# Two edits to a hybrid attention layer: table copies at another place, softmax reciprocals on another engine

## The chip, the cores and the metric

The kernel runs on one core of a Trainium2 chip. A core has a matrix engine (TensorE, PE in the profile, with its weight loads on a row of their own, PEld), three engines for elementwise work (VectorE, DVE; ScalarE, ACT; GpSimd, POOL) and a queue that issues transfers (SyncE, SP). The engines run side by side, each through its own instructions in a fixed order, and wait for each other by semaphores. Operands lie in an on-chip memory of 128 partitions. Matmul results go to a small memory of their own, PSUM, which the kernel uses as eight banks of 128 x 512 numbers. GpSimd does not touch PSUM in this kernel.

The metric is the time of one execution on the device in microseconds, as the median of the runs.

## The reference

Two decoder layers over 512 tokens of width 1024. Each layer projects its input once, and the columns feed two groups of heads and an indexer. Cut to what matters here:

```python
h = x @ w_in
qa, ka, va, qb, kb, vb, qi, ki, wi = split(h)
qa, ka, qb, kb, qi, ki = rope(...)            # ki after a layer norm of its own
# group A: window of 128 keys, a learned sink per head in the sum
m  = max(s.max(-1), sink)
pr = exp(s - m)
denom = pr.sum(-1) + exp(sink - m)
oa = einsum(pr / denom, v)
# group B: an index score picks 128 keys per query, then a softmax over these
idx_score = sum_h(relu(qi . ki) * wi), causal
sel = top_k(idx_score, 128)
ob = softmax(s over sel) @ v
mix = concat(oa, ob) @ w_o
x = layer_norm(alpha * x + mix)
x = layer_norm(alpha * x + (silu(x @ wg) * (x @ wu)) @ w_down + sigmoid(x @ w_pg) * (p @ w_pp))
```

`rope` turns pairs of columns by the cosine and sine of position times frequency. There are 8 query heads in each group, 8 index heads, and 2 layers.

## The kernel before

All matmuls are made of three products of a number split in two parts (high times high, high times low, low times high: `mm3`, L332 to L336). So every weight tile that arrives by a transfer (`wst`) is split before use: ScalarE rounds it to the high part (L256, L280, L287) and GpSimd subtracts that to get the low part (L257, L281, L288). The split tiles `wsp` have five buffers, and when TensorE is done with one (`w_rel`), the next is split and the next transfer issued (`w_pump`).

The tokens are four blocks of 128, `t` = 0 to 3. A layer runs through these stages:

- `start()` (L845): for each `t` the 296 columns of the indexer are projected (L865), and `gi_out` (L564) turns and splits the index queries and normalises the index key. Then the 384 key and value columns for blocks (0, 1) and (2, 3) (L868, `kv_out` at L605). Then `turned_tables()` (L869, L627). Then the first two query groups of A, `queries` (L833), whose results `q_out` (L640) turns with the turned tables.
- beside it `index()` (L670): for `t` = 1 to 3 and each of eight heads one product (L677), a relu on ScalarE (L679) and a weighted sum on VectorE (L680).
- then `rest()` (L873): the query groups of B and the first half of the output projection, beside `attention()` (L785) and `topk()` (L685, 16 rounds of the eight largest, L691 and L692, for each `t` from 1).
- the output projection's other half, the feed-forward part and the gated embedding, up to the next layer.

**The table copies.** The rotary table `tab64` holds, for each token (on partitions), 32 cosines and 32 sines, twice each. It is made once, at the start, by `rotary()` (L462 to L500). The queries come out of TensorE with columns on partitions, so each layer needs the table turned. `turned_tables()` copies for cosine and for sine the 32 columns four times side by side for each block (`wide`, L632, ScalarE, 128 x 512), turns the four blocks on TensorE into a PSUM bank (L636) and copies that to `cs` (L637). `wide` is one of the twelve buffers of the pool `t2k`. `cs` is read first by `q_out` (L645).

**The reciprocals.** `scores()` (L698) handles one unit: a group, a block `t` and four heads. After the products (L716), VectorE adds the mask and takes the negative maximum (L720), and ScalarE takes the exponential with its sum into `sums`, 128 x 4 (L724). For group A GpSimd makes the sink's exponent (L727), ScalarE its exponential (L728), and GpSimd adds it to `sums` (L729). Then VectorE takes the reciprocal (L730) and GpSimd copies it out to 64 columns per head (`rb`, L732). `values()` (L735) turns the exponentials (L753, copied by L755), multiplies by the values (L747), turns `rb` (L764, copied by L767) and multiplies the two (L772). `AHEAD = 2`: the values of a unit stand beside the scores of the unit two later. There are 16 units in a layer.

**What sets the order.** The Python program emits the work of each stage as several generators that `Order.run` (L67) interleaves by written-out costs. `order.later` puts transposes some cost units behind what feeds them (`D_K = 8.0` for the keys, L620 and L622; `D_GI` for the index queries, L532 and L533). The framework then takes the emitted instructions with their place in the program as priority, assigns buffers and banks (`bank`, L113: eight, shared by all), and fixes for each engine the order in which it runs its instructions. So an instruction emitted earlier may be put earlier on its engine, but at run time each engine goes through its list in order. `tc.issue_after` ties some to others.

Of the kernel before, what the change touches and what calls it, by code (L numbers as in the profile page):

```python
# [10 lines left out]
F32 = mybir.dt.float32  # L11
# [4 lines left out]
OP = mybir.AluOpType  # L16
# [4 lines left out]
NT = S // 128  # L21
# [75 lines left out]
def hybrid_kernel(ctx: ExitStack, tc: tile.TileContext, x, p, positions, ln_in_g, ln_in_b, w_in,  # L97
# [3 lines left out]
    PE, V, A, G, SP = nc.tensor, nc.vector, nc.scalar, nc.gpsimd, nc.sync  # L101
# [6 lines left out]
    small = ctx.enter_context(tc.tile_pool(name="small", bufs=4))  # L108
# [4 lines left out]
    def bank(tag, bufs, dt=F32):  # L113
        return psum.tile([128, 512], dt, name="bank", tag="bank", bufs=8)

    def acc():
        return bank("acc", 4)
# [4 lines left out]
    def t2k(dt=F32):  # L122
        return tmp.tile([128, 512], dt, name="t2k", tag="t2k")
# [23 lines left out]
    idf = const.tile([128, 128], F32, name="idf")  # L147
# [74 lines left out]
    def w_dma(i):  # L222
        if wq[i][0] == "op":
            return
        if wq[i][0] == "raw":
            _, w, f = wq[i]
            for q in ("11", "12", "21", "22"):
                h = int(q[1]) - 1
                quarter[q] = [slot(F32) for _ in range(2)]
                for j in range(2):  # L230
                    r = (2 * (f + j) + int(q[0]) - 1) * 128
                    SP.dma_start(quarter[q][j], w[r:r + 128, h * 512:(h + 1) * 512])
            return
        a, cols, _ = wq[i]
        n = sum(ap.shape[1] for ap in cols)
        st = wst.tile([128, 1024], F32, name="wst", tag="wst")
        sv = st[:, :a * n].rearrange("p (a n) -> p a n", a=a)
        o = 0
        for ap in cols:
            SP.dma_start(sv[:, :, o:o + ap.shape[1]], ap.rearrange("(a p) n -> p a n", p=128))  # L240
            o += ap.shape[1]
        wst_live[i] = st
        if i in X_AT:
            load_x(X_AT[i])
# [59 lines left out]
    def w_pump():  # L304
        while True:
            go = False
            staged = sum(e[0] != "op" for e in wq[wpos["split"]:wpos["dma"]])
            if wpos["dma"] < len(wq) and staged < ST_AHEAD:
                w_dma(wpos["dma"])
                wpos["dma"] += 1  # L310
                go = True
            i = wpos["split"]
            if i < wpos["dma"] and (wpos["room"] or wq[i][0] == "raw" or wq[i][2] is True and wq[i][0] != "op"):
                w_split(i)
                wpos["split"] += 1
                go = True
            if not go:
                return

    def w_take():  # L320
        i = wpos["use"]
        if wq[i][0] == "raw":
            i += 1
        wpos["use"] = i + 1
        assert i in w_live, (i, wpos)
        return w_live.pop(i)

    def w_rel():
        wpos["room"] += 1
        w_pump()  # L330
# [21 lines left out]
    for i in range(4):  # L352
        ps = bank("gb", 4)
# [3 lines left out]
    def tok(t):  # L357
        return slice(t * 128, (t + 1) * 128)
# [95 lines left out]
    tab64 = const.tile([128, NT, 2, 64], F32, name="tab64")  # L454
# [7 lines left out]
    def rotary():  # L462
# [33 lines left out]
        for tab, f0, h in ((tab64, 0, 32), (tab32, 32, 16)):  # L496
# [2 lines left out]
            A.copy(tab[:, :, 1, :h], s3[:, :, f0:f0 + h])  # L499
            G.tensor_scalar(tab[:, :, 1, h:], s3[:, :, f0:f0 + h], -1.0, 1.0, op0=OP.mult, op1=OP.mult)  # L500

    w_pump()
    ln_in(0)
    table = rotary()
# [36 lines left out]
    def take(n):  # L541
        return [w_take() for _ in range(n)]

    def project(ws, n, blocks, lhs, done, rel=0):

        ks = [(i, r, len(w[0])) for i, w in enumerate(ws) for r in range(len(w[0]))]
        ps = [acc() for _ in blocks]
        for k, (i, r, a) in enumerate(ks):
            for o, t in zip(ps, blocks):
                mm3(o[:, :n], *lhs(t, k), ws[i][0][r], ws[i][1][r], k == 0, k == len(ks) - 1)  # L550
            if i < rel and r == a - 1:
                w_rel()
            yield 3 * len(blocks) * 0.218 * n / 512
        for o, t in zip(ps, blocks):
            done(t, o)

    for l in range(L):
# [1 line left out]
        kiT = slot()  # L559
        qiT, qT, work, wi, vt, ma = {}, {}, {}, {}, {}, {}  # L560
        ready = set()
        kin, kmv, turned = {}, {}, []

        def gi_out(t, ps):  # L564

# [39 lines left out]
        def kv_out(t, ps):  # L605
# [18 lines left out]
                order.tick(0.4)  # L624
            order.later(D_K, turns)

        def turned_tables():  # L627

            cs = const.tile([128, D], F32, name="lng", tag="lng")
            for i in range(2):  # L630
                wide = t2k()
                A.copy(wide.rearrange("p (t n i) -> p t n i", t=NT, n=4),  # L632
                       tab64[:, :, i, None, :32].to_broadcast([128, NT, 4, 32]))
                ps = bank("tp", 2)
                for t in range(NT):
                    PE.transpose(ps[:, tok(t)], wide[:, tok(t)], idf)  # L636
                A.copy(cs[:, i * 512:(i + 1) * 512], ps)  # L637
            return cs[:, :512], cs[:, 512:]

# [58 lines left out]
        def scores(kind, t, g, st):  # L698
            if kind == "a":
                k0, nk, c = max(0, t - 1) * 128, (256 if t else 128), g  # L700
                mask = win if t else win[:, 128:]
                yield from wait((kind, t, g), *[("k", b) for b in range(max(2, t + 1))])
            else:
                k0, nk, c = 0, (t + 1) * 128, 2
                yield from wait((kind, t, g), *[("k", b) for b in range(max(2, t + 1))], *[("s", t)] * (t > 0))
                mask = work[t] if t else causal[:, S - 128:]
            nn = max(nk, 256)
            per = 512 // nn
            ng, sums = sm(4, "ng"), sm(4, "sums")
            es = []  # L710
            for j in range(4):
                if j % per == 0:
                    ps, e = bank("sc", 2), t2k()
                o = j % per * nn
                for s in range(2):
                    PE.matmul(ps[:, o:o + nn], qT[kind, g][j][:, tok(t)], kT[c, s][:, k0:k0 + nn],  # L716
                              start=(s == 0), stop=(s == 1))
                es.append(e[:, o:o + nk])
                far = nsink[:, l, 4 * g + j:4 * g + j + 1] if kind == "a" else 3e38
                V.tensor_tensor_reduce(es[j], ps[:, o:o + nk], mask, -HD ** -0.5, far, op0=OP.add, op1=OP.min,  # L720
                                       accum_out=ng[:, j:j + 1])
                yield 0.44 * nn / 512
            for j in range(4):
                A.activation(es[j], es[j], AF.Exp, bias=ng[:, j:j + 1], scale=-1.0, accum_out=sums[:, j:j + 1])  # L724
            if kind == "a":
                ek = sm(4, "ek")
                G.tensor_tensor(ek, sink[:, l, 4 * g:4 * g + 4], ng, OP.add)  # L727
                A.activation(ek, ek, AF.Exp)  # L728
                G.tensor_tensor(sums, sums, ek, OP.add)  # L729
            V.reciprocal(sums, sums)  # L730
            rb = small.tile([128, 256], F32, name="rb", tag="rb", bufs=3)
            G.tensor_copy(rb.rearrange("p (j d) -> p j d", j=4), sums[:, :, None].to_broadcast([128, 4, 64]))  # L732
            st.extend([es, rb, k0 // 128, nk // 128])
# [111 lines left out]
        def start():  # L845
            ws = take(3)
            for t in range(NT):
                if l == 0 or t == 3:
                    to_features(t)
                    yield 0.9  # L850
                if l == 0 and t == 0:
                    with tc.issue_after(last["copy"]):
                        ln_in_sums(2)
                    ln_in_sums(3)
                    for _ in table:
                        pass
                if l == 0 and t + 1 < NT:
                    ln_in(t + 1)
                done = gi_out
                if l == 0 and t + 1 < NT:  # L860
                    done = behind(last["norm"], gi_out)
                if l == 0 and t == 2:
                    with tc.issue_after(last["norm"]):
                        V.tensor_scalar(nsink, sink, -1.0, None, op0=OP.mult)
                yield from project(ws, 296, (t,), from_f, done, 3 * (t == 3))  # L865
            ws = take(4)
            for b in ALL:
                yield from project(ws, 384, b, from_f, kv_out, 4 * (b is ALL[-1]))  # L868
            turned.extend(turned_tables())  # L869
            for q in QS[:NSTART]:  # L870
                yield from queries(*q)
# [133 lines left out]
        for gi, fs in enumerate(GROUPS):  # L1005
            hs = []
            for f in fs:
# [7 lines left out]
                if gi == 1 and f == fs[0]:  # L1015
                    pT = {}
                    for k in range(2):
                        ps = bank("tp", 2)
# [14 lines left out]
            for h in range(2):  # L1033
                ps = [acc() for _ in range(NT)]
                n = len(hs)
# [13 lines left out]
        for b in TAIL:  # L1049
            for h in range(2):  # L1050
# [4 lines left out]
                ps = [acc() for _ in b]  # L1055
# [52 lines left out]
```

## Time and profile before

| | us |
|---|---|
| median of 3 runs | 1276.74 (1276.61 to 1277.25) |
| the profiled execution's own time | 1275.16 |
| its span in the profile | 1273.4 |
| TensorE busy in the span | 1223.8 |
| GpSimd busy in the span | 677.9 |

The profile shows one execution; times in it are microseconds from the start of its span. A row of its timeline gives start, duration, engine, line of the kernel, operation, output and inputs, shapes and count (neighbouring instructions of one kind are merged), and in brackets how long the engine was idle before and what it waited for. A row of the table by stretches gives for each engine the busy time and the number of instructions, then the granted TensorE clock (1.00 is full), the share of the transfer engines and what they moved. A table of waits gives who waited for whom, the total, how often, and the longest. A row for a line of the kernel gives the shortest, median and longest duration of its instructions in ns, and when the first and the last started. Matmuls overlap, so their durations are longer than the distance from one to the next.

### The profile page before, as it was taken

To read this page: it belongs to the slowest core of one execution; us is meant where nothing else is said; L and a number is where in the kernel's file an instruction comes from. 1 tells how busy PE (TensorE), PEld (TensorE's weight loads), DVE (VectorE), ACT (ScalarE), POOL (GpSimd) and SP (SyncE) were. 2 spreads that over 40 slices of the span, in tenths; PEclk is the share of its full clock that TensorE was granted. 3 is DMA by queue.
4 is the path that set the end of the run, shared out by engine and by line. 5 is a ranking of instruction groups with operands and counts; after the bars stand their busy time and mean duration, and the time that the engine had idled before them with its cause. 6 is when DMAs were issued, how large, how long until landed. Compare 5 with 4: busy or idle time off the path is not lost.

```text
span 1273.4 us, 17210 instructions
## 1 busy us (share of the span) xinstructions
PE 1223.8 (96%) x6056; PEld 1006.3 (79%) x6056; DVE 773.4 (61%) x1678; ACT 583.4 (46%) x1185; POOL 677.9 (53%) x523
## 2 busy tenths in 40 slices
PE   7889999999999999999997989999999999999996
PEld 5877667888888888888896867679888888888885
DVE  7689953773636363726677997556736363645365
ACT  6557774443434343434335766843434342434331
POOL 6856632366565656562166645324756575747400
PEclk9989999999999999999998989999999999999998
DMA  5324241343242323034032433204242423231321
GB/s 174 85 82 118 76 155 35 99 131 115 69 132 74 125 77 121 17 116 138 13 91 79 126 90 92 108 27 155 85 132 67 132 79 120 84 99 42 108 83 50
DMA packets 95406, 121.09 MB, mean 95 GB/s; under 512 B 7508, under 2 KB 68180, under 8 KB 95320
## 3 DMA queue, kind: packets, MB, share of 16 engines
q1 hardware_dynamic: 94648, 119.97, 30.4%
q8 instruction: 47, 0.77, 0.3%
q14 instruction: 39, 0.32, 0.1%
q10 hardware_dynamic: 672, 0.03, 0.0%
HBM read 109.49 MB, written 2.10 MB: 88 GB/s over the span
## 4 chain that ended last, share of the span: by engine, by line
PE 83%; DVE 5%; ACT 4%; POOL 4%; issue 2%; DMA 2%; SPq 0%; DVEq 0%; ACTq 0%; POOLq 0%
PE bank L334 25%; PE bank L335 25%; PE bank L336 25%; PE bank L747 2%; PE bank L716 2%; PE bank L753 2%; DMA wst<-in_w_pg_dram 1%; POOL wsp L288 1%; POOL wsp L281 1%; DVE t2k L720 1%; ACT t2k L724 1%; POOL slot L526 1%; PE bank L447 1%; DVE slot L273 1%; PE bank L764 1%
## 5 line engine op out<-in xcount | busy, mean ns | idle before, releaser
L288 POOL TENSOR_TENSOR wsp<-wst,wsp 128x1024 fp32r<-128x1024 f32 (+2 forms) x132 | 313.1, 2385 | 252.2 <-ACT wsp L287 250.2
L335 PE MATMUL bank<-fl,wsp 128*128 128x512 f32 (+1 forms) x896 | 336.0, 376 | 0.4 <-DVE fl L450 0.4
L334 PE MATMUL bank<-fh,wsp 128*128 128x512 f32 (+1 forms) x896 | 335.1, 377 | 1.0 <-ACT fh L449 1.0
L336 PE MATMUL bank<-fh,wsp 128*128 128x512 f32 (+1 forms) x896 | 334.2, 375 | 0.0
L287 ACT CAST wsp<-wst 128x1024 fp32r<-128x1024 f32 (+2 forms) x132 | 134.8, 1030 | 181.2 <-PE bank L336 132.7
L334 PEld LDWEIGHTS bank<-fh,wsp 128*128 128x128 f32 x896 | 168.5, 189 | 31.6 <-ACT fh L449 1.9
L335 PEld LDWEIGHTS bank<-fl,wsp 128*128 128x128 f32 x896 | 169.4, 189 | 30.0 <-DVE fl L450 0.9
L336 PEld LDWEIGHTS bank<-fh,wsp 128*128 128x128 f32 x896 | 169.3, 189 | 29.7
L914 DVE TENSOR_TENSOR t2k<-bank,t2k 128x512 f32<-128x512 f32 x44 | 30.4, 692 | 222.2 <-PE bank L336 222.2
L257 POOL TENSOR_TENSOR wsp<-slot,wsp 128x512 fp32r<-128x512 f32 x100 | 141.4, 1440 | 28.9 <-ACT wsp L256 28.9
L334 PE MATMUL bank<-wsp,slot 128*128 128x512 f32 x392 | 153.3, 391 | 0.0
L335 PE MATMUL bank<-wsp,slot 128*128 128x512 f32 x392 | 152.7, 390 | 0.0
L336 PE MATMUL bank<-wsp,slot 128*128 128x512 f32 x392 | 148.0, 389 | 0.0
L822 DVE TENSOR_TENSOR x<-bank,x 128x512 f32<-128x512 f32 x140 | 91.5, 686 | 88.5 <-PE bank L336 88.5
L944 ACT CAST slot<-t2k 128x256 fp32r<-128x256 f32 (+1 forms) x104 | 49.9, 498 | 143.7 <-DVE t2k L914 102.1
L257 POOL TENSOR_TENSOR wsp<-t2k,wsp 128x512 fp32r<-128x512 f32 x40 | 57.5, 1449 | 92.7 <-ACT wsp L256 92.7
L334 PE MATMUL bank<-wsp,fh 128*128 128x512 f32 (+2 forms) x256 | 92.2, 364 | 1.1 <-ACT fh L449 0.8
L336 PE MATMUL bank<-wsp,fl 128*128 128x512 f32 (+2 forms) x256 | 91.4, 360 | 1.5 <-DVE fl L450 0.8
L335 PE MATMUL bank<-wsp,fh 128*128 128x512 f32 (+2 forms) x256 | 91.5, 357 | 0.0
L334 PEld LDWEIGHTS bank<-wsp,slot 128*128 128x128 f32 x392 | 73.6, 188 | 15.8 <-issue 0.8
L336 PEld LDWEIGHTS bank<-wsp,slot 128*128 128x128 f32 x392 | 73.6, 188 | 15.3
L335 PEld LDWEIGHTS bank<-wsp,slot 128*128 128x128 f32 x392 | 73.6, 188 | 15.0
(163 smaller groups left out, 1971.7 us busy)
## 6 DMA issues: line engine op xcount, KB each, us to landing
wst<-in_w_gu_dram SPq DMA_DIRECT2D x88, 512.0 KB, 3.5
slot<-in_w_down_dram SPq DMA_DIRECT2D x80, 256.0 KB, 2.9
wst<-in_w_in_dram SPq DMA_DIRECT2D x16, 512.0 KB, 3.5
wst<-in_w_o_dram SPq DMA_DIRECT2D x16, 512.0 KB, 3.9
slot<-t2k SPq DMA_DIRECT2D x128, 64.0 KB, 2.0
wst<-in_w_pg_dram SPq DMA_DIRECT2D x16, 512.0 KB, 4.1
wst<-in_w_in_dram SPq DMA_DIRECT2D x8, 256.0 KB, 2.9
lng<-in_ln_g_dram SPq DMA_DIRECT2D x4, 512.0 KB, 3.9
```

Source lines behind the costliest of these rows:

```text
L257: G.tensor_tensor(w[:, 1, j], src[j], w[:, 0, j], OP.subtract)
L287: A.copy(w[:, 0, :a * n], st[:, :a * n])
L288: G.tensor_tensor(w[:, 1, :a * n], st[:, :a * n], w[:, 0, :a * n], OP.subtract)
L334: PE.matmul(o, sh, mh, start=start, stop=False, skip_group_check=again)
L335: PE.matmul(o, sh, ml, start=False, stop=False, skip_group_check=again)
L336: PE.matmul(o, sl, mh, start=False, stop=stop, skip_group_check=again)
L716: PE.matmul(ps[:, o:o + nn], qT[kind, g][j][:, tok(t)], kT[c, s][:, k0:k0 + nn], start=(s == 0), stop=(s == 1))
L747: PE.matmul(o[u * 64:(u + 1) * 64], vt[b0 + b][:, c * 64:(c + 1) * 64], pts[b][:, u], start=b == 0, stop=b == nb - 1)
L753: PE.transpose(ps[:, j * 128:(j + 1) * 128], es[j][:, b * 128:(b + 1) * 128], idf)
L822: V.tensor_tensor(xt[t][:, c], ps, xt[t][:, c], OP.add)
L914: V.tensor_tensor(a, ps[1, f], a, OP.mult)
L944: A.copy(h[0], src)
```

## The change

Three things are edited.

- The two copies to `wide` leave `turned_tables()` and become a function `wide_tables()`, which `start()` calls when the indexer's projection of `t` = 1 is done. The tiles are kept in a list until `turned_tables()` turns them. The transposes L636 and the copies L637 stay where they were.
- The reciprocal of `sums` is no longer VectorE's `reciprocal` but a GpSimd `tensor_tensor` with the operation `pow`, and a second operand that holds −1 everywhere.
- That operand, `less_one`, 128 x 4, is written once by GpSimd at the start.

```diff
@@ -499,6 +499,8 @@
             A.copy(tab[:, :, 1, :h], s3[:, :, f0:f0 + h])
             G.tensor_scalar(tab[:, :, 1, h:], s3[:, :, f0:f0 + h], -1.0, 1.0, op0=OP.mult, op1=OP.mult)
 
+    less_one = small.tile([128, 4], F32, name="less_one", tag="less_one", bufs=1)
+    G.memset(less_one, -1.0)
     w_pump()
     ln_in(0)
     table = rotary()
@@ -559,7 +561,7 @@
         kiT = slot()
         qiT, qT, work, wi, vt, ma = {}, {}, {}, {}, {}, {}
         ready = set()
-        kin, kmv, turned = {}, {}, []
+        kin, kmv, turned, wide = {}, {}, [], []
 
         def gi_out(t, ps):
 
@@ -624,16 +626,20 @@
                 order.tick(0.4)
             order.later(D_K, turns)
 
+        def wide_tables():
+
+            for i in range(2):
+                wide.append(t2k())
+                A.copy(wide[i].rearrange("p (t n i) -> p t n i", t=NT, n=4),
+                       tab64[:, :, i, None, :32].to_broadcast([128, NT, 4, 32]))
+
         def turned_tables():
 
             cs = const.tile([128, D], F32, name="lng", tag="lng")
             for i in range(2):
-                wide = t2k()
-                A.copy(wide.rearrange("p (t n i) -> p t n i", t=NT, n=4),
-                       tab64[:, :, i, None, :32].to_broadcast([128, NT, 4, 32]))
                 ps = bank("tp", 2)
                 for t in range(NT):
-                    PE.transpose(ps[:, tok(t)], wide[:, tok(t)], idf)
+                    PE.transpose(ps[:, tok(t)], wide[i][:, tok(t)], idf)
                 A.copy(cs[:, i * 512:(i + 1) * 512], ps)
             return cs[:, :512], cs[:, 512:]
 
@@ -727,7 +733,7 @@
                 G.tensor_tensor(ek, sink[:, l, 4 * g:4 * g + 4], ng, OP.add)
                 A.activation(ek, ek, AF.Exp)
                 G.tensor_tensor(sums, sums, ek, OP.add)
-            V.reciprocal(sums, sums)
+            G.tensor_tensor(sums, sums, less_one, OP.pow)
             rb = small.tile([128, 256], F32, name="rb", tag="rb", bufs=3)
             G.tensor_copy(rb.rearrange("p (j d) -> p j d", j=4), sums[:, :, None].to_broadcast([128, 4, 64]))
             st.extend([es, rb, k0 // 128, nk // 128])
@@ -863,6 +869,8 @@
                     with tc.issue_after(last["norm"]):
                         V.tensor_scalar(nsink, sink, -1.0, None, op0=OP.mult)
                 yield from project(ws, 296, (t,), from_f, done, 3 * (t == 3))
+                if t == 1:
+                    wide_tables()
             ws = take(4)
             for b in ALL:
                 yield from project(ws, 384, b, from_f, kv_out, 4 * (b is ALL[-1]))
```

## The prediction

> **What bounds the kernel now.** I read the page's first part, then the table of waits for TensorE over the whole run.
>
> ```profile
> span 1273.4 us, 17210 instructions
> ...
> PE 1223.8 (96%) x6056; PEld 1006.3 (79%) x6056; DVE 773.4 (61%) x1678; ACT 583.4 (46%) x1185; POOL 677.9 (53%) x523
> ```
>
> ```profile
> engine line waited for: us in total, times, longest us
> PE bank L636 <- ACT t2k L632: 16.1, 2, 8.4
> PE bank L764 <- POOL rb L732: 6.8, 3, 3.8
> ```
>
> TensorE is busy 1223.8 of 1273.4 us. So the kernel is a chain of matmuls, and what can be won is its 49.6 us of idle time and whatever the clock loses beside it. The two waits shown hold 22.9 us of that, and the change touches both: L632 is the copy of the rotary table, and L732 stands right behind the reciprocal L730. Next I read the timeline around the first wait, in layer 0 (start, duration, engine, line; in brackets the idle time before and what ended it).
>
> ```profile
> 57.29 1.13 PE L620 MATMUL bank<-idr,slot 128*128 128x128 f32 x12
> 58.81 2.12 ACT L622 CAST slot<-bank 128x128 fp32r<-128x128 f32 x12
> 59.64 4.67 POOL L281 TENSOR_TENSOR wsp<-wst,wsp 128x1024 fp32r<-128x1024 f32 x2
> 65.30 0.82 ACT L525 CAST slot<-t2k 128x128 fp32r<-128x128 f32 x2 [2.23 <-POOL t2k L522]
> 66.18 1.14 ACT L632 COPY t2k<-tab 128x512 f32<-128x512 f32 x2
> 66.86 1.97 PE L636 MATMUL bank<-idf,t2k 128*128 128x128 f32 x8 [8.44 <-ACT t2k L632]
> 67.23 0.21 ACT L613 COPY slot<-bank 128x64 f32<-128x64 f32 x1
> 68.48 0.78 PE L334 MATMUL bank<-fh,wsp 128*128 128x512 f32 x1
> ```
>
> TensorE finishes the key transposes at 58.42 and stands 8.44 us. It wants the widened table, whose copies need only a table made long before. But the copies stand on ScalarE behind L525, which waits for GpSimd's L522, and GpSimd spends 59.64 to 64.31 on two weight splits. The first query matmul starts at 68.48. Layer 1 has the same picture:
>
> ```profile
> 679.97 2.12 ACT L622 CAST slot<-bank 128x128 fp32r<-128x128 f32 x12
> 688.40 1.97 PE L636 MATMUL bank<-idf,t2k 128*128 128x128 f32 x8 [7.71 <-ACT t2k L632]
> 688.76 0.21 ACT L613 COPY slot<-bank 128x64 f32<-128x64 f32 x1
> 690.02 0.78 PE L334 MATMUL bank<-fh,wsp 128*128 128x512 f32 x1
> ```
>
> Last, the table by stretches of time (us, busy time and count of PE, PEld, DVE, ACT, POOL, then granted clock, DMA share, GB/s), for the clock and for who else is full:
>
> ```profile
> 61.50:62.00 0.50, 0.00 (x0) 0.00 (x0) 0.47 (x2) 0.50 (x3) 0.50 (x2) 0.51 1.09 389
> 66.86:71.50 4.64, 4.64 (x15) 4.07 (x16) 4.30 (x14) 1.95 (x5) 0.80 (x3) 0.50 0.11 40
> 692.50:693.00 0.50, 0.50 (x3) 0.40 (x2) 0.47 (x2) 0.00 (x0) 0.00 (x0) 0.53 0.00 0
> 58.40:150.00 91.60, 79.47 (x417) 62.29 (x416) 84.00 (x257) 65.08 (x186) 52.87 (x61) 0.93 0.36 104
> 680.70:772.00 91.30, 78.16 (x400) 61.77 (x402) 85.12 (x249) 62.10 (x172) 51.37 (x59) 0.91 0.35 101
> 112.00:197.00 85.00, 81.00 (x464) 58.99 (x465) 64.37 (x211) 63.62 (x189) 37.78 (x55) 0.98 0.33 102
> ```
>
> The idle time costs twice: the clock falls to half at about 61.5, and the queries still run at half clock at 71.5. In layer 1 it comes back just before 693.0 (0.53 over the half microsecond before).
>
> **The change, part by part. The copies.** Per layer two ScalarE copies move to a much earlier place: no DMA, and the same tile size.
>
> ```profile
> L632 ACT COPY t2k<-tab x4: 621/622/622, 66.2 to 688.2; 128x512 f32<-128x512 f32 x4
> 28.40 1.60 ACT L449 CAST fh<-bank 128x512 fp32r<-128x512 f32 x3
> 36.48 0.84 ACT L287 CAST wsp<-wst 128x768 fp32r<-128x768 f32 x1 [6.47 <-PE bank L336]
> ```
>
> The transposes L636 and their evictions L637 stay where they are. Once the wide table lies ready, what is late next? PSUM. At 58.42 all eight banks are taken: two by the last key/value products (read until 67.23 + 0.21 = 67.44), four by the key transposes, two by index products. L622 empties the four at 58.81 + 2.12 = 60.93 at the latest. The two table transposes and the two query accumulators need four banks, so by 60.93 all can start (the weight halves that the first queries use are split by then or soon after), and I put the first query matmul there.
> - Layer 0: 68.48 − 60.93 = **−7.55**.
> - Layer 1: 690.02 − (679.97 + 2.12) = **−7.93**.
>
> The clock: layer 1 runs ordinary matmuls at half clock from 690.02 to 693.0, and half of these 3.0 us, **−1.5**, would go, since the gap left there is 1.4 us (688.40 − 7.71 = 680.69 to 682.09), and in layer 0 the clock fell only some 3 us into the gap (58.42 to 61.5). In layer 0 I count **0** (bounds 0 and −1.5): without ordinary matmuls from 57.29 to 60.93, 3.6 us, it may still fall. That rests on taking transposes as idle, and the rows say so: the eight of L636 began at 66.86 and 688.40, but the clock was at half until 3.0 us or more after the first ordinary matmul, 68.48 and 690.02.
> The Trainium skill, "TensorE: Matmul & The Clock Gate", Part 4 (PE-mode transpose), says the same against this change: a transpose does not count as TensorE being busy. With transposes as busy time, layer 0 would win another 1.5 us and the sum be −16.0; by the page's rule it is the one I use, and the trace agrees.
>
> Against this gain stand three costs.
> - The index products L677 run between the queries. Two banks are left for them while the key/value banks are held until 67.44, and their evictor ScalarE idles behind L525 until 65.30. Below, 0 if they are evicted in that hole; above, about 2.9 (the third, due near 65.5, waiting until 68.4). I take 0.6 per layer, nearer to zero because the hole of 2.23 us is empty: **+1.2**.
> - In layer 0 the table itself is finished just before the three L449 casts of 28.40, for which TensorE waits. Two copies of 0.62 ahead of these cost 1.24; behind them, in the 6.47 us hole before 36.48, nothing. I take half: **+0.6**. In layer 1 the table is old; 0. Two of twelve t2k buffers are held some 30 us longer; no row shows a rope waiting for a buffer, so 0, inside the range if the cover goes.
> - VectorE is nearly full behind the gap: 84.00 of 91.60 us in layer 0, 85.12 of 91.30 in layer 1. While TensorE stands, it runs the first top-k rounds as filler. If all of that had to be done before TensorE passes the end of the stretch, TensorE could come forward only 7.6 and 6.2 us, plus some ten reciprocals of 0.17. But the last top-k is wanted only after these stretches. So below 0, above about 3 (9.3 of layer 1 cut to 7.8, some blocking in layer 0); I take **+1.0**.
>
> **The reciprocals.** Thirty-two VectorE instructions become thirty-two on GpSimd, which now runs add, power and broadcast copy in a row, without leaving the engine.
>
> ```profile
> L730 DVE RECIPROCAL sums<-sums x32: 148/173/179, 112.0 to 819.8; 128x4 f32<-128x4 f32 x32
> L729 POOL TENSOR_TENSOR sums<-sums,ek x16: 192/200/203, 111.8 to 770.8; 128x4 f32<-128x4 f32 x16
> 5.68 0.35 POOL L471 TENSOR_SCALAR t2k<-t2k 128x192 f32<-128x192 f32 x1
> 6.12 0.87 POOL L472 TENSOR_SCALAR t2k<-t2k 128x192 f32<-128x192 f32 x1
> 146.53 0.20 POOL L729 TENSOR_TENSOR sums<-sums,ek 128x4 f32<-128x4 f32 x1
> 147.99 0.40 POOL L732 COPY rb<-sums 128x256 f32<-128x256 f32 x1 [1.25 <-DVE sums L730]
> 734.20 0.20 POOL L729 TENSOR_TENSOR sums<-sums,ek 128x4 f32<-128x4 f32 x1 [0.74 <-ACT ek L728]
> 735.25 0.74 POOL L732 COPY rb<-sums 128x256 f32<-128x256 f32 x2 [0.24 <-DVE sums L730]
> ```
>
> No row shows a power. From below: 0.20, an add of the same shape. From above: 2.33, half of the L281 pair, as if four elements cost what 1024 do. The operation does matter on this engine (0.35 against 0.87 at one shape), so I take 0.2 × 2.5 = 0.5, near the same-shape row. Then a copy starts 0.2 + 0.5 after L729: at 147.23 instead of 147.99, and at 734.90 instead of 735.25, −1.1 together. Where VectorE was prompt, 0.5 in place of 0.17 brings the copy 0.3 later: two or three times where TensorE waits for it, +0.8. Net **−0.3**. The freed 5.5 us of VectorE are in the DVE term. The other 26 or so lie two attention units ahead of their use and cost nothing unless the power takes several us. The memset of −1 is one small GpSimd instruction at the start: 0.
>
> Sum: −7.55 − 7.93 − 1.5 + 1.2 + 0.6 + 1.0 − 0.3 = **−14.5 us**. The profiled execution took 1275.16 (span 1273.4 and 1.8 around it), 1.6 below the median of 1276.74. It goes to 1260.7, the median to **1262.2**. TensorE being 377.56 of 378.00 us busy from 248 to 626 (the same table), nothing behind absorbs a lead.
>
> ```profile
> 248.00:626.00 378.00, 377.56 (x1715) 314.25 (x1714) 196.72 (x283) 141.03 (x216) 209.06 (x116) 1.00 0.30 94
> ```
>
> **Rivals.**
> 1. *Half of it.* The third index product waits for a bank until 68.4 in each layer: 2 × 2.3 less won, −9.9, **1267**. For it: full PSUM. Against: the hole on ScalarE.
> 2. *The wait is replaced or stays.* The queries get the key/value banks (67.44, and 688.76 + 0.21 = 688.97) or the copies still stand late, since the order on ScalarE is fixed at compile time: 1.04 + 1.05 or nothing, **1275 to 1277**. Against: four other banks are free by 60.93.
> 3. *The power is slow* (the slower side). Place: GpSimd, between sum and copy. In 112 to 197 it has 85.00 − 37.78 = 47.2 us free for 16 powers, so it is full at 2.95 us each. Up to there the four places where TensorE takes the copy at once (the three waits of the first table and the one behind 147.99) cost 4 × 2.45 = 9.8, which leaves −4.7; beyond, every further us costs 32. It decides at about 3.1 us; at 4 us the time is 1276.7 − 4.7 + 33.6 = **1306**. For it: only that no row shows one; against: the smallest GpSimd rows stand at 0.2.
> 4. *The first power loads code.* ScalarE shows a load of its own, 1.28 below; on GpSimd it would hold the first unit's copy, for which TensorE waits: once +1.3, **1263.5**.
> 5. *More.* The start of attention waits for that same copy and then runs cold in both layers (rows below). If the earlier order dissolves both: 2.26 + 3.81 idle, 3.78 × 0.45 = 1.7 and 5.60 × 0.46 = 2.6 of clock, up to −10.4 on top, **1252**. Against: what delays the sums there is a weight split on GpSimd and a full VectorE, and neither goes.
>
> ```profile
> 103.61 1.28 ACT L724 ACT_TABLE_LOAD   x1
> 112.72 0.69 PE L764 MATMUL bank<-idf,rb 128*128 128x128 f32 x2 [2.26 <-POOL rb L732]
> 112.72:116.50 3.78, 3.78 (x17) 2.80 (x18) 3.48 (x12) 3.62 (x10) 0.79 (x3) 0.55 0.59 176
> 735.70 0.69 PE L764 MATMUL bank<-idf,rb 128*128 128x128 f32 x2 [3.81 <-POOL rb L732]
> 733.92:741.30 7.38, 5.60 (x26) 4.48 (x28) 7.24 (x24) 4.62 (x15) 1.88 (x5) 0.54 0.41 144
> ```
>
> The Trainium skill, "GPSIMD Engine Reference", Instruction dispatch, puts the first call of a freshly loaded kernel at 5.95 us, with no instruction to be seen in a profile. If the power were such a call, rival 4 would stand at 1268.2 instead; no run here shows one.
>
> **How the numbers follow.** Forecast 0.45; half 0.15; replaced or not done 0.11; slow power 0.08; code load 0.05; more 0.16. From 1252 to 1274 lie the forecast with its bounds, 1, 4 and nearly all of 5, about 0.8. Some 0.2% (2.6 us) is what a measurement can tell from no change: faster 0.84, the same 0.08 (most of rival 2), slower 0.08.
>
> **What will show it.** L636 no longer waiting for L632; the first query matmul at about 61 and 682; no half clock after it in layer 1; a power row on GpSimd of about 0.5 us. Wrong: a bank or index wait of several us in L636 or L677, a power above 2 us, or TensorE's idle time in the attention stage grown by what was won.

## The result and the profile after

| | before | after |
|---|---|---|
| median, us | 1276.67 (1275.01 to 1277.25, 4 runs) | 1266.38 (1265.99 to 1268.33, 4 runs) |
| the profiled execution's own time | 1275.16 | 1268.33 |

The ratio is 0.9925, with a 95% interval of 0.9907 to 0.9942. So the change wins 10.3 us, where 14.5 were forecast. The profiled execution of after is the slowest of its four, and that of before is below its median. Differences between the two traces therefore come out some 3.5 us smaller than the medians say (6.83 against 10.29).

First the page of after (span; busy us of each engine, with its share and its instructions), then its table of waits for TensorE over the whole run.

```profile
span 1266.6 us, 17231 instructions
...
PE 1223.9 (97%) x6056; PEld 1006.5 (79%) x6056; DVE 764.9 (60%) x1646; ACT 583.2 (46%) x1185; POOL 710.1 (56%) x556
```

```profile
PE bank L770 <- POOL rb L738: 12.3, 6, 4.4
```

The wait for the widened table, 16.1 us before, is not among them. But the other wait that the change touches has grown: L770 and L738 are the lines L764 and L732 of before, and there it was 6.8 us at three places. GpSimd is busy 32.2 us more (710.1 against 677.9), and VectorE 8.5 us less. VectorE lost 32 reciprocals of 0.173, 5.5 us.

The timeline of after around the two places where TensorE stood before (L633 is L632 of before, L642 is L636, L624 is L622):

```profile
28.23 1.60 ACT L449 CAST fh<-bank 128x512 fp32r<-128x512 f32 x3
29.72 1.14 ACT L633 COPY t2k<-tab 128x512 f32<-128x512 f32 x2
...
58.67 2.12 ACT L624 CAST slot<-bank 128x128 fp32r<-128x128 f32 x12
59.32 1.09 PE L642 MATMUL bank<-idf,t2k 128*128 128x128 f32 x8 [1.04 <-DVE work L686]
60.17 0.47 PE L334 MATMUL bank<-fh,wsp 128*128 128x512 f32 x1
...
678.56 2.12 ACT L624 CAST slot<-bank 128x128 fp32r<-128x128 f32 x12
679.40 1.17 PE L642 MATMUL bank<-idf,t2k 128*128 128x128 f32 x8 [0.76 <-ACT slot L624]
680.33 0.47 PE L334 MATMUL bank<-fh,wsp 128*128 128x512 f32 x1
```

The reader is to see three things. The copies in layer 0 run right behind the three casts, not ahead of them. The table transposes now wait only about 1 us, for banks: for the index sum L686 and for the key casts. And the first query matmul follows the start of the key casts by 1.50 us (60.17 − 58.67) and 1.77 us, where it took 9.67 (68.48 − 58.81) and 10.05 (690.02 − 679.97). That is 8.17 and 8.28 us won at the two places. Where before ran its first queries at half clock, after has the full clock (stretches of its time; PE busy, granted clock, DMA share, GB/s):

```profile
61.50:71.50 10.00, 10.00 (x52) 1.00 0.45 133
680.33:693.00 12.67, 12.67 (x65) 1.00 0.43 125
```

**Where the lead went.** I follow four events through the layers: the first turn of `rb` in each layer (the first attention unit), and the first transpose of the mixed heads, L447, behind each attention stage. For before the two turns stand in the prediction, at 112.72 and 735.70. Here is the timeline of before, then of after:

```profile
228.73 1.03 PE L447 MATMUL bank<-idf,x 128*128 128x128 f32 x8
...
852.55 1.03 PE L447 MATMUL bank<-idf,x 128*128 128x128 f32 x8
```

```profile
104.55 0.44 PE L770 MATMUL bank<-idf,rb 128*128 128x128 f32 x2 [3.93 <-POOL rb L738]
...
227.29 1.03 PE L447 MATMUL bank<-idf,x 128*128 128x128 f32 x8
...
725.31 0.69 PE L770 MATMUL bank<-idf,rb 128*128 128x128 f32 x2 [4.38 <-POOL rb L738]
...
845.67 1.03 PE L447 MATMUL bank<-idf,x 128*128 128x128 f32 x8
```

After leads before by 8.17 us at the first turn, by 1.44 at the end of the first attention stage, by 10.39 at the first turn of layer 1, and by 6.88 at the end. So the two fronts (all that lies ahead of a layer's first turn, the wait for it included) win 8.17 + 8.95 = 17.1 us, and the two attention stages give back 6.73 + 3.51 = 10.2. Behind the end the lead hardly changes: 6.83 us in the executions' own times.

The two attention stages of before and then of after (length, PE busy, granted clock, DMA share, GB/s) show what the 10.2 us are:

```profile
112.72:228.73 116.01, 112.73 (x634) 0.99 0.27 84
735.70:852.55 116.85, 113.62 (x634) 0.98 0.25 79
```

```profile
104.55:227.29 122.74, 117.14 (x633) 0.94 0.25 78
725.31:845.67 120.36, 114.48 (x633) 0.97 0.25 76
```

TensorE's idle time grows by 5.0 us (6.5 to 11.5), and its busy time for the same matmuls by 5.3, at a lower clock. The fronts are mostly the copies' part. What the attention stages give back is the question for the experiments.

The power is the first suspect. Its row (shortest, median, longest in ns):

```profile
L736 POOL TENSOR_TENSOR sums<-sums,less_one x32: 1006/1008/1049, 102.5 to 813.0; 128x4 f32<-128x4 f32 x32
```

It takes 1.008 us for four numbers per partition, twice what I took, and five times the add of the same shape. The first one, which starts at 102.5, lies with all others between 1006 and 1049, so no load of code shows in it. The Trainium skill, "GPSIMD Engine Reference", Instruction dispatch, puts 5.95 us at the first call of freshly loaded code. The trace doesn't show it here: the first power, in a row further down, took 1.05 us with no idle time named ahead of it.

### The profile page after: what moved, and what is told of

It reads as the page before. It is cut to its first block, busy times and chain, and to the rows that moved or that the text cites. A ratio compares the mean times of both kernels' runs of the same rounds, so it can differ in the third digit from the quotient of the medians.

```text
span 1266.6 us, 17231 instructions
## 1 busy us (share of the span) xinstructions
PE 1223.9 (97%) x6056; PEld 1006.5 (79%) x6056; DVE 764.9 (60%) x1646; ACT 583.2 (46%) x1185; POOL 710.1 (56%) x556
## 4 chain that ended last, share of the span: by engine, by line
PE 79%; DVE 5%; POOL 4%; ACT 4%; issue 3%; DMA 3%; SPq 2%; DVEq 0%; ACTq 0%; POOLq 0%
PE bank L334 24%; PE bank L335 24%; PE bank L336 24%; PE bank L753 2%; PE bank L722 2%; DMA wst<-in_w_pg_dram 2%; PE bank L759 2%; POOL wsp L288 2%; SPq L661 2%; ACT t2k L730 1%; DVE m L697 1%; DVE work L698 1%; DMA wst<-in_w_in_dram 1%; POOL slot L528 1%; PE bank L447 1%
## 5 line engine op out<-in xcount | busy, mean ns | idle before, releaser
L952 ACT CAST slot<-t2k 128x256 fp32r<-128x256 f32 (+1 forms) x104 | 49.8, 497 | 144.1 <-DVE t2k L922 102.5
L335 PEld LDWEIGHTS bank<-wsp,slot 128*128 128x128 f32 x392 | 73.6, 188 | 15.2
```

The lines of the kernel that those rows point to most:

```text
L335: PE.matmul(o, sh, ml, start=False, stop=False, skip_group_check=again)
L952: A.copy(h[0], src)
```

## The experiments

Two theories stood at the start. **P**: the power costs what the attention stage gave back, because it lengthens the chain from the sums to the first turn. **V**: VectorE's unfinished choice of keys takes back part of what the copies win, whatever the reciprocal is. All edits are against the kernel after, but where before is named.

### The two parts alone

The copies alone (`e1_copies`):

```diff
-            G.tensor_tensor(sums, sums, less_one, OP.pow)
+            V.reciprocal(sums, sums)
```

> The copies moved, the reciprocals back on VectorE. Theory P (the power, 1.01 us on GpSimd in the path from the sum to the broadcast copy, gives the lead back in the attention stage): 1258 to 1262 us, TensorE's waits for the broadcast copy at or under the 6.8 us of the kernel before. Theory V (the attention stage swallows the lead whatever makes the reciprocal, since VectorE is full there): 1265 to 1268 us, like the changed kernel.

Measured 1258.35 us (1257.36 to 1258.79), 0.9854 of before (0.9841 to 0.9868): 18.2 us won, not 14.2 as the terms of the copies had it.

The power alone, against before (`e2_pow`):

```diff
+    less_one = small.tile([128, 4], F32, name="less_one", tag="less_one", bufs=1)
+    G.memset(less_one, -1.0)
...
-            V.reciprocal(sums, sums)
+            G.tensor_tensor(sums, sums, less_one, OP.pow)
```

> The power alone, the copies at their old place. Theory P: slower than before, 1278 to 1285 us, with TensorE waiting some 10 to 13 us for the broadcast copy. Theory V: 1275 to 1278 us, no change.

Measured 1282.34 us (1280.77 to 1283.43), 1.0043 of before (1.0030 to 1.0055): the power costs 5.7 us by itself. Beside the copies it costs 8.0 (1266.38 − 1258.35). Both results stand on the side of P, although TensorE waits somewhat longer for the copied sums than P had it: 7.2 us in the copies alone (at most 6.8 expected) and 15.2 with the power alone (10 to 13 expected). The same four events in the timeline of the copies alone:

```profile
104.03 0.69 PE L768 MATMUL bank<-idf,rb 128*128 128x128 f32 x2 [2.84 <-POOL rb L736]
...
221.99 1.03 PE L447 MATMUL bank<-idf,x 128*128 128x128 f32 x8
...
718.49 0.69 PE L768 MATMUL bank<-idf,rb 128*128 128x128 f32 x2 [3.97 <-POOL rb L736]
...
835.82 1.03 PE L447 MATMUL bank<-idf,x 128*128 128x128 f32 x8
```

The leads over before are 8.69, 6.74, 17.21 and 16.73 us: the fronts win 8.69 + 10.47 = 19.2, and the attention stages give back only 1.95 + 0.48 = 2.4. The power alone, in turn:

```profile
113.48 0.69 PE L766 MATMUL bank<-idf,rb 128*128 128x128 f32 x2 [3.20 <-POOL rb L734]
...
232.94 1.03 PE L447 MATMUL bank<-idf,x 128*128 128x128 f32 x8
...
739.72 0.69 PE L766 MATMUL bank<-idf,rb 128*128 128x128 f32 x2 [5.48 <-POOL rb L734]
...
859.29 1.03 PE L447 MATMUL bank<-idf,x 128*128 128x128 f32 x8
```

It is 0.76, 4.21, 4.02 and 6.74 us late. So it loses 3.45 and 2.72 us within the two attention stages, and little elsewhere.

### Is it the power's length, its place, or GpSimd's time?

Three powers in a row, which give the same result as one (`e4_pow3`):

```diff
-            G.tensor_tensor(sums, sums, less_one, OP.pow)
+            for _ in range(3):
+                G.tensor_tensor(sums, sums, less_one, OP.pow)
```

> The changed kernel with the power taken three times in a row (the sum to the power of -1, of -1 and of -1 again, which is the reciprocal still): 2.0 us more on GpSimd for each of 32 units, 64.5 us in all. Theory P: about six waits of TensorE grow by 2 us each and more clock is lost, 1277 to 1295 us. Theory V: within 4 us of the changed kernel, up to 1270 us.

Measured 1320.72 us (1319.46 to 1321.48), 1.0343 of before (1.0329 to 1.0357). That is 54 us for two more powers, and more than either theory had. TensorE's wait for the copied sums (total, times, longest):

```profile
PE bank L771 <- POOL rb L739: 55.4, 14, 9.4
```

64 more powers of 1.008 us are 64.5 us, so most of their length arrives in the time. Yet GpSimd is not full: it is busy 85.26 of the 143.13 us of the first attention stage (108.55 to 251.68).

An unread power behind each copy of `rb`, and VectorE's reciprocal in its old place (`e5_beside`):

```diff
-            G.tensor_tensor(sums, sums, less_one, OP.pow)
+            V.reciprocal(sums, sums)
...
+            idle = sm(4, "idle")
+            G.tensor_tensor(idle, sums, less_one, OP.pow)
```

> The copies moved, the reciprocals on VectorE, and a power of the same size into a tile that nobody reads behind each broadcast copy, so that GpSimd carries the 32 us of powers but no chain does. If the power costs by its delay in the chain: within 2 us of the kernel with the copies alone. If it costs by the time of GpSimd that it takes: 1264 to 1268 us, like the changed kernel. Theory V: also 1264 to 1268 us.

Measured 1259.70 us (1259.03 to 1260.21), 0.9864 of before (0.9849 to 0.9879), within 1.4 us of the copies alone. The table of lines shows that the 32 powers ran:

```profile
L740 POOL TENSOR_TENSOR idle<-sums,less_one x32: 1005/1008/1238, 103.8 to 805.5; 128x4 f32<-128x4 f32 x32
```

So GpSimd has 32 us to spare; what costs is the power between the sum and the copy.

A product by −1 on the same tiles at the same place (`e10_product`):

```diff
-            G.tensor_tensor(sums, sums, less_one, OP.pow)
+            G.tensor_tensor(sums, sums, less_one, OP.mult)
```

> The changed kernel with a product by minus one on GpSimd in the place of the power, on the same tiles, behind the same sum: the reciprocal is left out of the computation. Theory D (the power costs by its own 1.008 us in the chain from the sums to the first turn of a unit): with an instruction of about the length of the sum beside it (0.20 us) the time is near that of the copies alone, 1255 to 1260 us, and the longest first waits of a unit for the turned sums fall from about 4 us to 3 or less. Theory Q (what costs is the place in GpSimd's queue, behind the next unit's sums, whatever the instruction there): 1263 to 1267.

Measured 1259.67 us (1259.08 to 1260.22), 0.9872 of before (0.9858 to 0.9885), in the range of theory D; the longest wait stays a little above the 3 us that D had. Its row and its wait:

```profile
L736 POOL TENSOR_TENSOR sums<-sums,less_one x32: 198/199/204, 103.0 to 804.2; 128x4 f32<-128x4 f32 x32
```

```profile
PE bank L770 <- POOL rb L738: 6.9, 4, 3.5
```

The engine and the operands are those of after. 0.81 us less per instruction takes 6.7 us off the time, and the wait falls from 12.3 to 6.9. What is left of the 8.0, 1.3 us, would be the step from VectorE to GpSimd; that is not shown, since the unread powers alone moved the time as much (1.4). One thing is not held fixed: the framework lays the engines' orders out anew for each kernel, and behind the first turn the two orders differ. So the 6.7 us are the longer instruction together with what the framework puts around it.

### Where it hurts

The first unit in the timeline of after, then of the copies alone:

```profile
102.23 0.21 POOL L735 TENSOR_TENSOR sums<-sums,ek 128x4 f32<-128x4 f32 x1
...
102.53 1.05 POOL L736 TENSOR_TENSOR sums<-sums,less_one 128x4 f32<-128x4 f32 x1
103.96 0.20 POOL L735 TENSOR_TENSOR sums<-sums,ek 128x4 f32<-128x4 f32 x1 [0.38 <-ACT ek L734]
104.10 0.40 POOL L738 COPY rb<-sums 128x256 f32<-128x256 f32 x1
```

```profile
102.80 0.21 POOL L733 TENSOR_TENSOR sums<-sums,ek 128x4 f32<-128x4 f32 x1
...
103.58 0.40 POOL L736 COPY rb<-sums 128x256 f32<-128x256 f32 x1 [0.43 <-DVE sums L734]
```

From the sum to the copy it takes 1.87 us with the power (102.23 to 104.10) and 0.78 without. The extra is not the power's length alone: the next unit's sum stands in GpSimd's order between power and copy, and waits 0.38 us for ScalarE there.

A unit of group B in the timeline of after, and the stretch that follows (PE busy, clock, DMA share, GB/s). Then the same unit with the product:

```profile
168.22 1.02 POOL L736 TENSOR_TENSOR sums<-sums,less_one 128x4 f32<-128x4 f32 x1 [4.71 <-ACT t2k L730]
...
169.21 0.72 POOL L786 TENSOR_TENSOR fl<-t2k,fh 128x256 fp32r<-128x256 f32 x1
...
169.88 0.40 POOL L738 COPY rb<-sums 128x256 f32<-128x256 f32 x1
...
170.33 0.69 PE L770 MATMUL bank<-idf,rb 128*128 128x128 f32 x2 [1.80 <-POOL rb L738]
```

```profile
170.33:177.50 7.17, 7.17 (x30) 0.56 0.42 159
```

```profile
166.64 0.20 POOL L736 TENSOR_TENSOR sums<-sums,less_one 128x4 f32<-128x4 f32 x1 [4.49 <-ACT t2k L730]
...
166.90 0.40 POOL L738 COPY rb<-sums 128x256 f32<-128x256 f32 x1
...
167.35 0.44 PE L770 MATMUL bank<-idf,rb 128*128 128x128 f32 x2 [0.33 <-POOL rb L738]
```

Here the copy starts 1.66 us after the power and 0.26 after the product: about the power's own 0.8 us more, and the 0.72 us of L786, which stands between them in one order and not in the other. TensorE waits 1.80 us in place of 0.33. Then it runs 7.17 us at a clock of 0.56; if all of this work goes by the clock, that is 7.17 × 0.44 = 3.2 us more. So a wait of under 2 us costs up to 5 here.

The power in group A only (`e7_pow_a`), and in group B only (`e8_pow_b`, with `"b"`):

```diff
-            G.tensor_tensor(sums, sums, less_one, OP.pow)
+            if kind == "a":
+                G.tensor_tensor(sums, sums, less_one, OP.pow)
+            else:
+                V.reciprocal(sums, sums)
```

> The changed kernel with the power in the 16 units of group A alone, VectorE's reciprocal in the 16 of group B. If the power costs wherever it stands in the chain: about half of the 8 us that the power adds to the copies, 1261 to 1264. Rival, that only group B's units are tight (there the copy is taken at once): 1258 to 1260.

> The same the other way round, the power in the 16 units of group B alone. If it costs in both groups: 1261 to 1264. Rival, that only group B's units are tight: 1264 to 1267.

Measured 1265.55 us (1264.37 to 1266.65; ratio 0.9912, 0.9898 to 0.9925) for A, and 1260.82 us (1259.11 to 1264.63; 0.9882, 0.9864 to 0.9900) for B. Against the copies alone that is 7.2 and 2.5 us. The first lies above what was expected, the second just below. The two make 9.7 us where both together cost 8.0: the units don't simply add up. Group A has the first unit of each layer, and a chain with one more step, the sink; that this is why it costs more is not shown. The trace of the power in B alone shows that the waits are not the whole price. There TensorE waits for the copied sums 12.2 us at six places, as much as in after (12.3 at six), and yet the time is 5.6 us less (9.2 between the two traces). The wait of the group B unit above is there too, with this stretch behind it:

```profile
167.34 0.44 PE L773 MATMUL bank<-idf,rb 128*128 128x128 f32 x2 [1.81 <-POOL rb L741]
```

```profile
167.34:177.50 10.16, 9.31 (x62) 1.00 0.37 142
```

After the same wait the clock holds. Over the whole run TensorE is busy 1216.2 us there and 1223.9 in after, for the same 6056 matmuls. So the sum of the waits does not tell the price; whether the clock falls behind them matters as much. The clock also varies within this one kernel: its four runs took 1259.11, 1259.49, 1262.14 and 1264.63 us at a granted clock of 0.997, 0.994, 0.990 and 0.988.

### How much of it is the clock

24 unread products ahead of the first turn of each layer, so that TensorE works where it waited, on the copies alone (`e6_warm`) and on the kernel after (`e13_pow_warm`):

```diff
             pr = bank("tp", 2)
+            if (kind, t, g) == ("a", 0, 0):
+                for _ in range(24):
+                    PE.matmul(pr[:, 256:], idr, kT[0, 0][:, :256], start=True, stop=True)
             for a in range(2):
                 PE.transpose(pr[:, a * 128:(a + 1) * 128], rb[:, a * 128:(a + 1) * 128], idf)
```

> The copies alone, and in each layer 24 products of 128 x 256 whose result nobody reads ahead of the first turn of the reciprocals in the attention stage, where TensorE waits 4 us and then runs some 7 us at half clock (3.4 us lost per layer). Theory C (a long wait costs twice, by itself and by the clock): the products fill some 2.7 us of the wait, the clock holds, 1252 to 1256 us against 1258.4 for the copies alone. Rival (the clock in the records is an effect of the wait and costs nothing of its own): 1257 to 1260. If the wait is not there in the new order: up to 5.4 us slower, 1264.

Measured 1255.86 us (1255.07 to 1256.86), 0.9839 of before (0.9826 to 0.9853): 2.5 us below the copies alone, in the range of theory C, and the fastest kernel of this study.

> The changed kernel with 24 unread products (128x256) on TensorE ahead of the first turn of each layer, where it waits for the first unit's sums: the result is the same. The same edit took the copies alone from 1258.35 to 1255.86. Theory C (about half of what the power costs is the clock that falls after the first wait of each layer; 1.7 us lost behind 104.55 and 3.4 behind 722 in the profiled run): the time falls by 4 to 7 us, to 1259.5 to 1262.5, so that the power costs 3.5 to 6.5 beside the same edit without it. Rival (the first waits are the lesser part; later ones and the order make up the cost): 1263 to 1266, so that it still costs some 8.

Measured 1264.11 us (1263.48 to 1266.82), 0.9910 of before (0.9897 to 0.9924): 2.3 us below after, and still 8.25 above the same edit without the power. My theory C falls: the cold stretch behind the first wait is not what makes the power dear. A later turn in the kernel after with the products, then in the copies with them:

```profile
785.30 0.56 PE L773 MATMUL bank<-idf,rb 128*128 128x128 f32 x2 [1.81 <-POOL rb L738]
```

```profile
779.58 0.44 PE L771 MATMUL bank<-idf,rb 128*128 128x128 f32 x2 [0.65 <-POOL rb L736]
```

With both first waits filled, the power is 0.45 us late at L447 behind the first attention stage (222.73 against 222.28) and 6.65 behind the second (841.00 against 834.35), where the turn shown waits 1.81 us against 0.65. Which places pay changes from kernel to kernel with the order and with the phase of the clock; beside the copies the sum is near 8 both times, and 5.7 without them.

Half clock remains a large part of it, only at other places. Between the traces of after and of the copies alone, idle time makes 5.0 us (42.7 against 37.7) and longer busy time 5.1 (1223.9 against 1218.8). Between the two traces with the products it is 1.2 us of idle and 5.8 of busy time (35.4 and 1226.7 against 34.2 and 1220.9); the one with the power runs three stretches of 3.41 us at half clock behind its first turn, the other has one such stretch.

### A reciprocal behind the turn

No reciprocal of `sums`; instead VectorE takes it from PSUM where ScalarE copied the turned sums, 128 x 256 (`e9_late`):

```diff
-            G.tensor_tensor(sums, sums, less_one, OP.pow)
...
-            A.copy(rr, pr[:, :256].rearrange("p (a n) -> p a n", a=2))
+            V.reciprocal(rr, pr[:, :256].rearrange("p (a n) -> p a n", a=2))
```

> The copies alone, but the sums themselves are copied out and turned, and VectorE takes the reciprocal of the turned 128 x 256 out of PSUM, in place of ScalarE's copy. No reciprocal stands before TensorE any more. If the queue on VectorE ahead of the small reciprocal is what is left of the wait, and a reciprocal of 256 elements takes about as long as other VectorE instructions of that size (some 0.45 us): 1252 to 1257. If it takes 2 us and more, 64 us of a nearly full VectorE: 1262 to 1280.

Measured 1267.50 us (1266.55 to 1267.65), 0.9928 of before (0.9916 to 0.9941). From the table of lines:

```profile
L770 DVE RECIPROCAL t2k<-bank 128x256 f32<-128x256 f32 x32 | 56.0, 1749 | 3.8 <-PE bank L767 3.6 <-ACT t2k L758 0.2
```

1.749 us for 256 numbers per partition, against 0.173 for four. That is near the 2 us of the second case, and the time lies in its range: what the shorter chain ahead of the turn wins is lost again. Whether by the length of the reciprocal behind the turn or by the 56 us of VectorE was not separated.

### VectorE's part

12 of the 16 rounds of the choice of keys, in the copies alone (`e11_copies_12`) and in before (`e12_before_12`):

```diff
-                for _ in range(TOPK // 8):
+                for _ in range(12):
```

> The copies alone, with 12 of the 16 rounds of the choice of keys (96 keys are picked and not 128). With VectorE's load lighter by a quarter of its choice of keys, theory V (VectorE's unfinished choice takes part of the copies' lead in the attention stage) has the copies worth 20 to 23 us against the kernel before with 12 rounds; the rival (VectorE takes nothing of it; the copies are worth what their removed wait was) has 17 to 19, as with 16 rounds (18.2).

> The kernel before with the same 12 of 16 rounds of the choice of keys (96 keys are picked and not 128); the base of the run above. Theory V: slower than the run above by 20 to 23 us; the rival: by 17 to 19.

Measured 1259.00 us (1258.95 to 1259.72) and 1282.00 us (1279.26 to 1282.49). The difference is 23.0 us, which theory V had. But it does not come as V has it: with less work for VectorE the copies' kernel is not faster (1259.00 against 1258.35), and before is 5.8 us slower with less work. Its order on TensorE differs from before's from the attention stage on. So the pair says nothing for V, and suggests instead that a new layout is worth several us here. The trace of before with 12 rounds has TensorE busy 1228.6 us in place of 1223.8 for the same number of matmuls, and idle 52.0 in place of 49.6, at a granted clock of 0.981 in place of 0.985; so most of the loss is slower matmuls. That the order brings it was not tried.

## Why the prediction was right, and where it was not

The time, 1266.4, lies in the range, 4.2 us above the forecast of 1262.2. That it is so close is luck: two misses partly cancel. The copies won 4 us more, and the reciprocals cost 8.3 us more.

- **What is late next (PSUM).** Right. L642 waits for banks, 1.04 and 0.76 us. The first queries stand at 60.17 and 680.33, forecast 60.93 and about 682. The terms −7.55 and −7.93 measure −8.17 and −8.28.
- **The clock behind the gap.** In layer 1 as forecast. In layer 0 I counted 0 and the clock held; the bound of −1.5 was the right end. Not all of this reached the end, since the first turn waits longer (3.93 us in place of 2.26).
- **Index products for want of a bank, +1.2.** Zero: TensorE is busy without a gap in both stretches shown, 61.5 to 71.5 and 680.33 to 693, where it was to wait.
- **Copies ahead of the casts of L449, +0.6.** Zero: they stand behind these casts.
- **VectorE full, +1.0.** The copies alone give back 2.4 us in the attention stages. The size is not far off, but that VectorE takes it is not shown; a lighter VectorE brought nothing. (Its upper bound starts from 9.3 us for layer 1, where the terms 7.93 and 1.5 make 9.4; nothing hangs on it.) What the trace shows is a first turn that waits 2.84 and 3.97 us in place of 2.26 and 3.81.
- **The reciprocals, −0.3.** This is the step that failed: +8.0 beside the copies, +5.7 alone. Two things were wrong in it. The size: I took 0.5 us "near the same-shape row", and the power takes 1.008. And the sentence that "the other 26 or so lie two attention units ahead of their use and cost nothing unless the power takes several us": with 0.5 us more than forecast at the places I named, the loss would be about 2 us. But the wait for the copied sums came up at six places instead of three, also in group B (170.33), and there a wait of 1.80 us brought some 3.2 us of half clock with it. The sum had no clock term for these waits at all. I counted the chain as add, power, copy in a row; in after the next unit's sum or the low part of an earlier unit's result (L786) stands between power and copy.
- **Rival 3, the slow power,** was right in its place and wrong in its price: it counted four places up to 2.95 us, where GpSimd would be full, so 4 us for each further us, and 32 beyond. For a power of 1.008 us that makes some 2 us. The runs show 6.7 us for the first 0.81 us more, and 54 us for the next 2.0, about 27 for each us, while GpSimd is busy 85 of 143 us. **Rival 4** (a code load) is out, **rivals 1 and 2** too. **Rival 5** did not come about: the first turns still wait in both layers. That they are worth something is shown by the 2.5 us that filling them brought.

One sign was named ahead that would speak against the forecast: TensorE's idle time in the attention stage growing by what was won. The lead lost there is 10.2 of 17.1 us, of which 2.4 come with the copies alone; 5.0 of the 10.2 are idle time, and the rest is matmuls that take longer. The sign named only the idle half.

## What to carry to other kernels

An operation that moves to another engine is to be priced in the chain it stands in, not by that engine's free time: the same 32 powers cost 1.4 us beside the chain and 8.0 within it. Before an unseen operation is taken at the price of its neighbour by shape, the forecast should be worked through at twice that price, at every place where the bounding engine takes the result at once. And where a change has two parts, each alone is the first run to make: here the copies without the power win 18.2 us, and the pair 10.3. A wait of TensorE is to be priced together with the clock behind it, and that price is uncertain: the same wait of 1.8 us cost some 3.2 us of clock in one kernel and none in another.

## What the runs showed of the hardware that was not expected

- A power on GpSimd takes 1.008 us for 128 x 4, and its length hardly varies (1006 to 1049 ns); a product on the same tiles takes 0.199. VectorE's reciprocal takes 0.173 us for 128 x 4 and 1.749 for 128 x 256 out of PSUM. If the memory makes no difference, which was not tried, that is some 6.3 ns for each further column.
- The clock fell to half with a wait of only 1.80 us (168.53 to 170.33). In stretches of after (PE busy, clock, DMA share, GB/s):

```profile
166.45:169.86 3.41, 1.90 (x14) 1.00 0.98 314
169.86:176.69 6.83, 6.36 (x25) 0.50 0.51 194
105.01:108.42 3.41, 3.41 (x16) 0.50 0.84 285
722.82:729.65 6.83, 4.34 (x19) 0.50 0.53 157
791.09:794.50 3.41, 3.41 (x15) 0.50 1.06 408
```

  The fall comes at 169.86, 1.33 us after TensorE's last work, and the return at 176.69, over 6 us after TensorE started again at 170.33. All half-clock stretches from the first turn to the end of the second attention stage last one or two times 3.41 us (the one not shown is 142.56 to 145.97). So half clock comes in whole steps here. One wait brings two of them and another none, like the wait of 1.81 us with the power in B alone; that it depends on where the wait lies among the steps is likely, but no run here shows it. The Trainium skill, "TensorE: Matmul & The Clock Gate", Part 1, gives an idle window of about 3.4 us for the fall and about 3.4 us of steady work for the return, in windows that run freely. The trace agrees on the steps and on the return, whose last step, 173.27 to 176.69, is the first that lies wholly behind the restart. It does not agree on the fall: TensorE was busy for 1.90 us of the step that ends at 169.86, more than 1 us of that with products that are no transposes, so no whole step of idleness was needed. What share of a step has to be idle no run here shows.
